# Placing three steps of a two-layer mLSTM and RG-LRU trunk by TensorE time, and turning one tile without DRAM

## The chip, the core and the metric

The kernel runs on one core of one Trainium2 chip. A core has a matrix engine (TensorE, PE in the profile), a vector engine (VectorE, DVE), an engine for pointwise functions (ScalarE, ACT), a general engine (GpSimd, POOL) and SyncE (SP), which here does nothing but issue transfers. Each engine works through its own queue in order. The metric is the device time of one execution in microseconds, as the median of several runs.

## The reference

The input `x` has 256 tokens of 2048 channels in float32. Two layers follow one another, then a root-mean-square norm. A layer does this:

```
u = rms_norm(x, norm_g);  p = u @ w_in            # 2048 -> 2048*6 + 16 columns
qk, v, o, z_a, ig, fg, xb, z_b = split(p)
qk = silu(causal_dwconv(qk, qk_conv))             # 4 taps along the tokens
h  = mlstm(q, k, v, ig, log_sigmoid(fg))          # 8 heads, dk 128, dv 256
h  = head_norm(h * sigmoid(o)) ;  y_a = h * silu(z_a)
xc = causal_dwconv(xb, lru_conv_w) + lru_conv_b
y_b = rg_lru(xc) * silu(z_b)                      # 8 blocks of 256 channels
x  = x + concat(y_a, y_b) @ w_out                 # 4096 -> 2048
```

In `mlstm` the weight of token s in the output at token t is (q_t . k_s) times exp(F_t - F_s + i_s - m_t), where F is the running sum of the log forget gate and m a running maximum; the sum over s is divided by max(|its sum without v|, exp(-m_t)). The kernel computes it over all 256 tokens at once, as a causal matrix of decays, `E`, times the scores. `rg_lru` makes two gates from `xc` by two block-diagonal products and then runs a linear recurrence h_t = a_t h_(t-1) + u_t along the tokens.

## The kernel before, in words

**Products.** All large products are weight streams. The weights lie in DRAM in blocks; a *unit* is 1 MB, a *half* 512 KB. For each half, SyncE loads a tile `raw` (128 x 1024), ScalarE casts it to `wH` (a rounded copy for the matrix engine), VectorE subtracts to get the rest `wL`, and TensorE multiplies the activations, themselves kept as a rounded part and a rest, in three products: rounded by rounded, rounded by rest, rest by rounded. A half of the ordinary kind is 12 matmuls of 128 x 128 by 512 columns. The loop at the end of `tile_trunk` goes over all halves in order; at half `n` it has prepared (cast and split) the halves up to `n + 3` (`AHEAD`). There are eight `raw` buffers (`SLOTS`) and four each of `wH` and `wL`. Some input products are done blockwise with sums of weights (`block_halves`, lines 1234 to 1236); their halves are 6 matmuls.

**Groups.** A layer goes in four groups `g` of two heads and 512 LRU channels. For each group the columns of q and k (`qk`), `v`, `o`, `z`, `xb` and `zb` are computed, then the two gate products of the LRU; the output product of a group comes while the next group is computed. In layer 1 the last group's output product is a function of its own, `last_out`: the rows of `w_out` in four quarters, of which the first two multiply `y_a` (lines 1357 to 1359 with `yaH`, `yaL`), the last two `y_b` (`ybH`, `ybL`). The third quarter's weights are cast into a tile of their own, `w_own`, and the casts are ordered behind those that make `ybH` and `ybL`.

**Turns.** The products give tokens on the partitions; the convolutions and the recurrence need channels there. `to_channels` copies a product into `tok` (ScalarE), `swapped` transposes it in 32 x 32 blocks into `blk` (VectorE, line 532), then four transfers issued by SyncE write it into a DRAM tile `moved` (line 535) in another order of blocks, and one transfer brings it back as `fr` (line 536). That one is issued by GpSimd, except for the last turn of all, `zb` of group 3 in layer 1, which SyncE issues: `zb_post` passes `back = nc.sync` there.

**The order of the work around the products.** Everything between the products is written as Python generators in a list `bg`. After each half the function `pump` goes through the list and asks each for its next step. A step yields its estimated cost, which is added to a lag; at a lag of 3 us (`FULL`) the pass ends. A generator that yields "wait" is passed over until the next pass. `st["t"]` counts the TensorE time of the halves so far, 2.72 us for an ordinary half and 1.36 us for a blockwise one, and `before(t)` is true until that clock has reached `t`. `require` runs steps by force when a product needs their result. So it is this clock that places a step between the casts and splits on ScalarE and VectorE; `order(...)` ties a step behind the newest cast or split. Within these ties, and those of the data, a scheduler of the framework settles the order on each engine, by its own estimate of when things are ready. Where an engine reaches an instruction whose input isn't there, it waits, and all that is queued behind it too.

The steps that the change touches:

- `e_gen` (lines 652 to 675) makes `E` of a group. It issues the transfer of two rows of `nG_d` to all partitions (`nb`, line 657, by GpSimd), yields "wait" four times, waits for `aT`, then lets VectorE add and clip (four instructions, lines 666 and 667), ScalarE take the exponential (line 669) and GpSimd set the upper triangle to zero (line 672).
- `qk_post` (from line 709): at least 10 us (`LANDING`) of TensorE time behind the turn, ScalarE copies `fr` to the tile `ch` (`joined`), the convolution runs over it (a ScalarE instruction and three on VectorE for each of four channel tiles, giving `qc`), a sigmoid and a product follow, and later the scores: products `ps_S` (lines 754 and 756) on TensorE, copied and added to `Pt`, times `E`. `Pt` lies in the buffer of `ch`; the flag `st["ch"]` says that it is in use. There are three small PSUM tiles (`aux`), and the scores of a head need two.
- `xb_post` (from line 838): the LRU channels, likewise at least 10 us behind their turn and when `ch` is free: `joined`, convolution to `xc`, and after the scores its cast and split.
- `zb_post` (line 933): the turned `zb` gives a sigmoid (`zsg`), two products and then `ybH` and `ybL`.

Of the kernel before, what the change touches and what calls it, by code (L numbers as in the profile page):

```python
# [22 lines left out]
NG = 4  # L23
# [3 lines left out]
O_NG, O_HG, O_QKW, O_LW, O_LB, O_BA, O_BX, O_LAM, NPAR = 0, 16, 32, 96, 160, 176, 192, 208, 224  # L27
AHEAD = 3
LANDING = 10.0
FAR = 15.0  # L30
BORDER = 7
BLANKS = 7
# [67 lines left out]
def tile_trunk(ctx, tc, x, xt, par, gw, gb, ws, final_g, out):  # L100
    nc = tc.nc
    G, PE = nc.gpsimd, nc.tensor
# [27 lines left out]
    st = {"nload": 0, "lag": 0.0, "dma": 0.0, "t": 0.0, "rate": RATE[0], "nprep": 0, "pair": 0, "aux": 0}  # L130
# [84 lines left out]
    def tt_(o, a, b, op):  # L215
        return V.tensor_tensor(out=o, in0=a, in1=b, op=op)
# [4 lines left out]
    def ts_(o, a, s1, op0, s2=None, op1=None):  # L221
        if s2 is None:
            return V.tensor_scalar(out=o, in0=a, scalar1=s1, scalar2=None, op0=op0)
        return V.tensor_scalar(out=o, in0=a, scalar1=s1, scalar2=s2, op0=op0, op1=op1)
# [45 lines left out]
    def order(ins, prev):  # L270
        tc.add_manual_dep(ins.ins, prev.ins.name,
                          mybir.DependencyInfo(mybir.DependencyClass.NoSync, mybir.DependencyReason.DATA),
                          reason="an order of the program")
# [28 lines left out]
    def before(t):  # L302
        return st["t"] < t and not st.get("forced")

    def pause(g, us, waits):
        t = st["t"] + us
        while before(t) if g < NG - 1 else waits > 0:
            waits -= 1
            yield "wait"
# [189 lines left out]
    def conv(x_, o, ct, wcol, l, bias):  # L499
        wv = pars[:, l, wcol : wcol + 4]  # L500
        if bias is None:
            S.activation(out=o[:, ct, :], in_=x_[:, ct, :], func=AF.Copy, scale=wv[:, 3:4])
        else:
            S.activation(out=o[:, ct, :], in_=x_[:, ct, :], func=AF.Identity, scale=wv[:, 3:4], bias=bias)
        for d in (1, 2, 3):
            stt(o[:, ct, d:T], x_[:, ct, 0 : T - d], wv[:, 3 - d : 4 - d], o[:, ct, d:T], ALU.mult, ALU.add)
# [8 lines left out]
    def to_channels(l, acc, back=G):  # L515
        require(("rstd", l))
        rstd = st["rstd", l]
        tok = new_tok()
        for t in range(2):
            S.activation(out=by_block(tok, t), in_=acc[:, t, :].rearrange("p (c m j) -> p c m j", c=4, m=4),  # L520
                         func=AF.Copy, scale=rstd[:, t : t + 1])
        return swapped(tok, back=back)

    def swapped(tok, blk=None, back=G):


        if blk is None:
            blk = work.tile([P, 4, 256], F32, tag="blk", name="blk")
        fr = work.tile([P, 4, 4, 2, 32], F32, tag="fr", name="fr", bufs=2)
        st["lag"] += 1.2  # L530
        st["dma"] += TURN
        V.transpose(out=blk.rearrange("p m n -> p (m n)"), in_=tok.rearrange("p m c t j -> p (m c t j)"))
        moved = dram.tile([P, 4, 256], F32, tag="moved", name="moved", bufs=2)
        for a in range(4):
            nc.sync.dma_start(out=moved[:, a].rearrange("(m j) n -> j m n", m=4), in_=blk[32 * a : 32 * a + 32])
        i0 = back.dma_start(out=fr.rearrange("p a c t i -> p a (c t i)"), in_=moved)  # L536
        if back is G:
            st["gq"] = i0
        return fr

    def pieces(fr):
# [15 lines left out]
    def joined(fr):  # L557
        ch = work.tile([P, 4, T], F32, tag="ch", name="ch")
        order(S.copy(out=whole(ch), in_=pieces(fr)), st["wH"])
        return ch  # L560
# [91 lines left out]
    def e_gen(l, g):  # L652
        while ("nG", l) not in st:
            yield "wait"
        nb = work.tile([P, 2, T], F32, tag="sD", name="nb")
        src = nG_d[l][2 * g : 2 * g + 2, :].rearrange("h t -> (h t)").partition_broadcast(P)
        st["nb", l, g] = nc.gpsimd.dma_start(out=nb.rearrange("p h t -> p (h t)"), in_=src)
        for _ in range(4):
            yield "wait"
        while ("aT", l) not in st:  # L660
            yield "wait"
        E = small.tile([P, 2, 384], F32, tag="E", name="E", bufs=1)
        aT = st["aT", l]
        for h in range(2):
            hd = 2 * g + h
            ts_(E[:, h, 0:256], nb[:, h, :], aT[:, 0, hd : hd + 1], ALU.add, 0.0, ALU.min)
            ts_(E[:, h, 256:384], nb[:, h, 128:256], aT[:, 1, hd : hd + 1], ALU.add, 0.0, ALU.min)
        yield 0.7
        order(S.activation(out=E, in_=E, func=AF.Exp), st["wH"])
        for h in range(2):  # L670
            for o in (0, 256):
                G.affine_select(out=E[:, h, o : o + 128], in_=E[:, h, o : o + 128], pattern=[[1, 128]],
                                compare_op=ALU.is_ge, fill=0.0, base=0, channel_multiplier=-1)
        st["E", l, g] = E
        yield 0.1
# [32 lines left out]

    def qk_post(l, g, acc):
        bg.append(e_gen(l, g))  # L710
        fr = to_channels(l, acc)
        relaxed = 0 < g < NG - 1
        t0 = st["t"]

        def gen():
            while before(t0 + LANDING) or st.get("ch"):
                yield "wait"
            st["turning"] = st["ch"] = True
            ch = joined(fr)
# [3 lines left out]
            for ct in range(4):  # L723
                conv(ch, qc, ct, O_QKW + 4 * (8 * (ct % 2) + 2 * g + ct // 2), l, None)
                yield 1.45
            st["ch"] = False
            if relaxed:
                yield "wait"
            order(S.activation(out=sg, in_=qc, func=AF.Sigmoid), st["wH"])
# [11 lines left out]
            st["turning"] = False  # L741
            yield 1.2
            yield from pause(g, 7.0, 3)
            while any((k, l, g) not in st for k in ("E", "v", "so")) or st["ch"]:
                yield "wait"
            st["ch"] = True
            E, em, so, (vH, vL) = st["E", l, g], st["em", l], st["so", l, g], st["v", l, g]
# [27 lines left out]
            for h in range(2):  # L775
                pns = [aux("ps_n") for _ in range(2)]
                for t in range(2):
                    o = pns[t][:, 0:258]
                    a = slice(P * t, P * t + P)
# [23 lines left out]
            st["hn", l, g] = hh  # L803
            yield 1.0
        bg.append(gen())

    def z_post(l, g, acc, sign="rstd"):
# [13 lines left out]
        def gen():  # L821
# [8 lines left out]
            t0 = st["t"]  # L830
            while before(t0 + (FAR if g < NG - 1 else LANDING)):
                yield "wait"
# [5 lines left out]
    def xb_post(l, g, acc):  # L838
        fr = to_channels(l, acc)
        t0 = st["t"]  # L840

        def gen():
            while before(t0 + LANDING) or st["ch"]:
                yield "wait"
            st["ch"] = True
            ch = joined(fr)
            yield 0.3
            xc = work.tile([P, 4, T], F32, tag="c4", name="xc", bufs=2)
            for ct in range(4):
                tix = 4 * g + ct  # L850
                conv(ch, xc, ct, O_LW + 4 * tix, l, pars[:, l, O_LB + tix : O_LB + tix + 1])
                yield 1.45
            st["ch"] = False
            while ("scores", l, g) not in st:
                yield "wait"
            xs = work.tile([P, 4, 2, T], F32R, tag="xcs", name="xcs")
            for b in range(2):
                sl_ = slice(2 * b, 2 * b + 2)
                S.copy(out=xs[:, sl_, 0, :], in_=xc[:, sl_, :])
                tt_(xs[:, sl_, 1, :], xc[:, sl_, :], xs.bitcast(F32)[:, sl_, 0, :], ALU.subtract)  # L860
                yield 0.6
            st["xc", l, g] = (xc, xs)
        bg.append(gen())
# [69 lines left out]
    def zb_post(l, g, acc):  # L933
# [4 lines left out]
        def gen():  # L938
            while not ending and before(t0 + FAR):
                yield "wait"  # L940
# [68 lines left out]
    def gate_before(l, g):  # L1009
        require(("xc", l, g))  # L1010
        if g == NG - 1:
            load_x_acc()

    def out_chunk(l, g, c):
# [9 lines left out]
        def postfn():  # L1024
# [27 lines left out]
            if c < 3:  # L1052
                tt_(xs, xs, ps, ALU.add)
            fr = swapped(tok, blk)
            square_sum(c)
            store_x(c)
# [391 lines left out]
    for item in dict.fromkeys(i for i, _ in seq):  # L1448
        kind, l, g = item[0], item[1], item[-1]
# [5 lines left out]
        elif kind == "gate":  # L1455
            add_unit([gate_half(l, g, 0), gate_half(l, g, 1)],
                     before=lambda l=l, g=g: gate_before(l, g), after=lambda l=l, g=g: gate_post(l, g))
# [6 lines left out]
    for item, j in seq:  # L1464
        l, what = item[1], item[2:]
        if _blockwise(item):
            p = next(p for p in range(PRODUCTS[l]) if what in PAIRS[p])
# [5 lines left out]
    for l in reversed(range(DEPTH)):  # L1473
        for p in reversed(range(PRODUCTS[l])):
            a, b = ends[l, p - 1], ends[l, p]
            if p == 1:
                g = PAIRS[1][1][1]
# [139 lines left out]
```

## Time and profile before

| | |
|---|---|
| median of 3 runs | 1478.61 us (1477.98 to 1481.65) |
| the profiled execution | 1479.07 us, of which 1477.2 us lie between its first and last instruction |
| TensorE busy | 1460.8 us (99%), 6734 matmuls |
| VectorE, ScalarE busy | 1213.1 us (82%), 981.5 us (66%) |
| GpSimd busy | 129.5 us (9%) |
| DMA | 417.06 MB, 282 GB/s on average |

In the rows of the profile, "L413" is line 413 of the kernel; where a helper records an operation its line stands for all of its callers (line 114 for nearly all of VectorE and ScalarE), so the tile names tell more: `acc<-wH,x_s` is a product of the tiles `wH` and `x_s` into `acc`. "x2" counts merged instructions. A figure in brackets, such as [2.75 <-DVE wL L114], is the time that the engine sat idle before the row, and what ended it. SPq and POOLq are the queues of SyncE and GpSimd. TensorE overlaps one matmul with the next, and the ends of matmuls are modelled: rows that are 0.39 us long may start 0.23 us apart.

### The profile page before, as it was taken

The numbers are of one execution on the slowest core, as the hardware profiler recorded it, in microseconds if no ns is written. First come the engines' busy times: TensorE is split into PE (matmuls) and PEld (weight loads), VectorE is DVE, ScalarE is ACT, GpSimd is POOL, SyncE is SP. The second block draws the span as 40 slices with busy tenths as digits, with TensorE's granted clock in tenths as the row PEclk, the third lists the DMA queues.
The fourth block names the chain that finished last, engine by engine and source line by source line (L and its number), as shares of the span: only waits on it lengthen the run. The fifth ranks groups of instructions, "written<-read, shape, count | busy, mean of one in ns | idle before, by whom it ended". The sixth has DMA issues, their size and how long they took to land.

```text
span 1477.2 us, 19595 instructions
## 1 busy us (share of the span) xinstructions
PE 1460.8 (99%) x6734; PEld 1217.2 (82%) x6734; DVE 1213.1 (82%) x1710; ACT 981.5 (66%) x1255; POOL 129.5 (9%) x210
## 2 busy tenths in 40 slices
PE   9999999999999999999999999999999999999997
PEld 7888888888888888888888788888888788888885
DVE  6888898878888699888857789988787877998875
ACT  7666766568676666668665577655677756667774
POOL 0020110110100000100100201111000000000002
PEclk9999999999999999999999999999999999999999
DMA  9979999999989998988998888999988899888891
GB/s 343 337 242 283 284 315 292 309 252 330 348 288 257 289 335 286 303 250 285 293 301 258 229 277 275 292 299 275 316 263 295 251 261 286 307 287 269 232 342 60
DMA packets 158708, 417.06 MB, mean 282 GB/s; under 512 B 14848, under 2 KB 35344, under 8 KB 158608
## 3 DMA queue, kind: packets, MB, share of 16 engines
q1 hardware_dynamic: 136432, 340.01, 67.7%
q0 software_dynamic: 19712, 71.33, 21.1%
q10 hardware_dynamic: 2464, 4.47, 0.8%
q8 instruction: 53, 0.87, 0.2%
q14 instruction: 47, 0.39, 0.1%
HBM read 378.50 MB, written 74.99 MB: 307 GB/s over the span
## 4 chain that ended last, share of the span: by engine, by line
PE 86%; DMA 6%; DVE 4%; issue 3%; ACT 1%; SPq 0%; POOL 0%; POOLq 0%; DVEq 0%; ACTq 0%
PE acc L413 68%; PE ps_b L1234 3%; PE ps_b L1236 3%; PE ps_b L1235 3%; PE ps_gt L879 3%; DMA raw<-in_ws_dram 2%; DMA fr<-moved 2%; PE acc L426 2%; DMA moved<-blk 1%; DVE wL L114 1%; DVE xc L114 1%; DVE qc L114 1%; PE acc L1358 1%; PE acc L1359 1%; PE acc L1357 1%
## 5 line engine op out<-in xcount | busy, mean ns | idle before, releaser
L114 DVE TENSOR_TENSOR wL<-raw,wH 128x1024 fp32r<-128x1024 f32 (+1 forms) x580 | 692.8, 1202 | 187.1 <-ACT wH L114 185.2
L114 ACT CAST wH<-raw 128x1024 fp32r<-128x1024 f32 (+1 forms) x580 | 597.2, 1039 | 356.1 <-PE acc L413 250.2
L413 PE MATMUL acc<-wH,x_s 128*128 128x512 f32 x2496 | 783.7, 389 | 0.0
L413 PEld LDWEIGHTS acc<-wH,x_s 128*128 128x128 f32 x2496 | 468.3, 188 | 97.6 <-ACT wH L114 1.1
L413 PE MATMUL acc<-wL,x_s 128*128 128x512 f32 x1248 | 484.7, 389 | 3.0 <-DVE wL L114 3.0
L413 PEld LDWEIGHTS acc<-wL,x_s 128*128 128x128 f32 x1248 | 234.3, 188 | 51.9 <-DVE wL L114 4.1
L413 PE MATMUL acc<-wL,ybH 128*128 128x512 f32 x224 | 87.3, 390 | 0.6 <-DVE wL L114 0.6
L413 PE MATMUL acc<-wH,ybL 128*128 128x512 f32 x224 | 87.5, 390 | 0.3 <-DVE ybL L989 0.3
L413 PE MATMUL acc<-wH,ybH 128*128 128x512 f32 x224 | 87.6, 391 | 0.0
L413 PE MATMUL acc<-wH,yaH 128*128 128x512 f32 x224 | 87.4, 390 | 0.0
L413 PE MATMUL acc<-wL,yaH 128*128 128x512 f32 x224 | 87.2, 389 | 0.0
L413 PE MATMUL acc<-wH,yaL 128*128 128x512 f32 x224 | 87.2, 389 | 0.0
L114 ACT ACT_TABLE_LOAD x62 | 79.5, 1283 | 5.1 <-DVE qc L114 2.7
L1141 POOL DMA_DIRECT2D w_d<-in_ws_dram x64 | 48.9, 765 | 292.8 <-ACT wH L114 265.4
L536 POOL DMA_DIRECT2D fr<-moved x34 | 19.2, 566 | 511.3 <-DMA moved<-blk 450.9
L114 DVE SCALAR_TENSOR_TENSOR xc<-ch,pars,xc 128x255 f32<-128x255 f32 (+2 forms) x96 | 42.3, 477 | 10.3 <-ACT xc L114 10.0
L1234 PE MATMUL ps_b<-wH,sums 128*128 128x512 f32 x128 | 50.1, 391 | 0.0
L413 PEld LDWEIGHTS acc<-wH,ybL 128*128 128x128 f32 x224 | 42.1, 188 | 9.7 <-DVE ybL L989 1.0
L1236 PE MATMUL ps_b<-wH,sums 128*128 128x512 f32 x128 | 49.9, 390 | 0.0
L1235 PE MATMUL ps_b<-wL,sums 128*128 128x512 f32 x128 | 49.9, 390 | 0.0
L413 PEld LDWEIGHTS acc<-wL,ybH 128*128 128x128 f32 x224 | 42.1, 188 | 9.3 <-DVE wL L114 0.9
L413 PEld LDWEIGHTS acc<-wH,yaL 128*128 128x128 f32 x224 | 42.0, 188 | 8.8
(229 smaller groups left out, 1763.2 us busy)
## 6 DMA issues: line engine op xcount, KB each, us to landing
raw<-in_ws_dram SPq DMA_DIRECT2D x542, 512.0 KB, 6.7
w_d<-in_ws_dram POOLq DMA_DIRECT2D x64, 512.0 KB, 9.1
raw<-w_d SPq DMA_DIRECT2D x48, 512.0 KB, 6.7
fr<-moved POOLq DMA_DIRECT2D x34, 512.0 KB, 7.3
moved<-blk SPq DMA_DIRECT2D x132, 128.0 KB, 3.9
x_d<-stage POOLq DMA_DIRECT2D x24, 512.0 KB, 7.9
x_d<-x_acc ACTq DMA_DIRECT2D x8, 512.0 KB, 7.8
w_d<-w_d POOLq DMA_DIRECT2D x8, 512.0 KB, 7.0
```

Of the source, the lines that this page charges most:

```text
L114: ins = f(*a, **k)
L413: st["mm"] = PE.matmul(o, a_[:, kt, P * t : P * t + P], W[:, k], start=b, stop=z)
L426: PE.matmul(ps[:, ct, T * part : 2 * T], W[:, k, P * ct : P * ct + P], moving, start=first and k == 0 and part == 0, stop=last and k == 3 ...
L536: i0 = back.dma_start(out=fr.rearrange("p a c t i -> p a (c t i)"), in_=moved)
L879: PE.matmul(o, W[:, ib, jl], xs[:, ib, a, :], start=j == 0 and i == 0 and W is Hv and a == 0, stop=i == 1 and W is Lv, skip_group_check=True)
L1141: i0 = G.dma_start(out=wd[l][p][to][j][:, cs], in_=(wd[l][p][src][j] if src == 0 else block_unit(l, p, *src, j))[:, cs], **how)
L1234: PE.matmul(box["b"], aH, Hv[:, k], start=opening and k == 0, stop=False, skip_group_check=True)
L1235: PE.matmul(box["b"], aH, Lv[:, k], start=False, stop=False, skip_group_check=True)
L1236: PE.matmul(box["b"], aL, Hv[:, k], start=False, stop=kp == 3 and k == 1, skip_group_check=True)
L1357: PE.matmul(o, yH[:, kt, tsl], Hv[:, k, cs], start=start and k == 0, stop=False)
L1358: PE.matmul(o, yH[:, kt, tsl], Lv[:, k, cs], start=False, stop=False)
L1359: PE.matmul(o, yL[:, kt, tsl], Hv[:, k, cs], start=False, stop=stop and k == 1)
```

## The change

There are four edits.

1. The four passes that `e_gen` waited become a wait by TensorE time: 10 us behind the issue of `nb`, 16 us in group 0.
2. When a convolution (of q and k or of the LRU channels) has been issued, the time is noted with 4 us added (`SETTLED`). In groups 0 to 2 the scores wait for that time.
3. The LRU channels' join and convolution of groups 1 and 2 begin 12.7 us behind their turn, not 10.
4. The last turn no longer goes through DRAM: 16 transfers, issued by SyncE, each take 32 partitions of 1 KB from `blk` straight to `fr`. All other turns stay as they were.

```diff
 LANDING = 10.0
+SETTLED = 4.0
...
         V.transpose(out=blk.rearrange("p m n -> p (m n)"), in_=tok.rearrange("p m c t j -> p (m c t j)"))
+        if back is not G:
+            for m in range(4):
+                for a in range(4):
+                    back.dma_start(out=fr[32 * m : 32 * m + 32, a].rearrange("p c t i -> p (c t i)"),
+                                   in_=blk[32 * a : 32 * a + 32, m])
+            return fr
         moved = dram.tile([P, 4, 256], F32, tag="moved", name="moved", bufs=2)
         for a in range(4):
             nc.sync.dma_start(out=moved[:, a].rearrange("(m j) n -> j m n", m=4), in_=blk[32 * a : 32 * a + 32])
-        i0 = back.dma_start(out=fr.rearrange("p a c t i -> p a (c t i)"), in_=moved)
-        if back is G:
-            st["gq"] = i0
+        st["gq"] = G.dma_start(out=fr.rearrange("p a c t i -> p a (c t i)"), in_=moved)
         return fr
...
         st["nb", l, g] = nc.gpsimd.dma_start(out=nb.rearrange("p h t -> p (h t)"), in_=src)
-        for _ in range(4):
-            yield "wait"
-        while ("aT", l) not in st:
+        t0 = st["t"]
+        while before(t0 + (LANDING if g > 0 else 1.6 * LANDING)) or ("aT", l) not in st:
             yield "wait"
...
-            st["ch"] = False
+            st["ch"], st["ch_t"] = False, st["t"] + SETTLED
             if relaxed:
                 yield "wait"
             order(S.activation(out=sg, in_=qc, func=AF.Sigmoid), st["wH"])
...
-            while any((k, l, g) not in st for k in ("E", "v", "so")) or st["ch"]:
+            while any((k, l, g) not in st for k in ("E", "v", "so")) or st["ch"] or g < NG - 1 and before(st["ch_t"]):
                 yield "wait"
...
-            while before(t0 + LANDING) or st["ch"]:
+            while before(t0 + (LANDING + 2.7 if 0 < g < NG - 1 else LANDING)) or st["ch"]:
                 yield "wait"
             st["ch"] = True
             ch = joined(fr)
...
-            st["ch"] = False
+            st["ch"], st["ch_t"] = False, st["t"] + SETTLED
             while ("scores", l, g) not in st:
                 yield "wait"
```

## The prediction

> **What bounds the kernel now.** I read the page first, then what TensorE (PE) waited for, then PE's timeline at each of those waits, and last the engine that each wait points to.
>
> ```profile
> PE 1460.8 (99%) x6734; PEld 1217.2 (82%) x6734; DVE 1213.1 (82%) x1710; ACT 981.5 (66%) x1255; POOL 129.5 (9%) x210
> ```
> ```profile
> PE acc L413 <- DVE wL L114: 3.6, 3, 2.8
> PE ps_S L754 <- DVE Pt L114: 1.5, 2, 0.8
> PE ps_blank L146 <- DVE blank L114: 1.3, 1, 1.3
> PE acc L1357 <- ACT w_own L114: 0.9, 2, 0.5
> PE acc_x L1357 <- ACT w_own L114: 0.4, 1, 0.4
> PE acc L413 <- DVE ybL L989: 0.3, 1, 0.3
> ```
>
> PE is busy for 99% of the span and the change takes no matmul away, so all that can be won is PE's own waiting: the rows (total, times, longest) sum to 8.0 us, of which 1.3 lie in the opening and 0.3 at a tile that the change leaves alone. PE's timeline shows where the rest is, and that a wait costs more than its idle figure.
>
> ```profile
> 826.40 0.61 PE L413 MATMUL acc<-wH,x_s 128*128 128x512 f32 x2
> 829.77 0.50 PE L413 MATMUL acc<-wL,x_s 128*128 128x512 f32 x1 [2.75 <-DVE wL L114]
> ```
> ```profile
> 445.00 0.39 PE L754 MATMUL ps_S<-qks 128*128 128x256 f32 x1 [0.76 <-DVE Pt L114]
> ```
> ```profile
> 1171.85 0.50 PE L413 MATMUL acc<-wL,ybH 128*128 128x512 f32 x1 [0.58 <-DVE wL L114]
> 1177.17 0.39 PE L754 MATMUL ps_S<-qks 128*128 128x256 f32 x1 [0.78 <-DVE Pt L114]
> ```
> ```profile
> 1444.14 0.39 PE L1358 MATMUL acc_x<-wL,yaH 128*128 128x512 f32 x1
> 1444.37 0.39 PE L1359 MATMUL acc_x<-wH,yaL 128*128 128x512 f32 x1
> 1445.17 0.49 PE L1357 MATMUL acc<-w_own,ybH 128*128 128x512 f32 x1 [0.41 <-ACT w_own L114]
> ```
>
> Undisturbed matmuls start 0.23 us apart (1444.14, 1444.37) though each is drawn 0.39 long, so an idle of g loses g + 0.16, and the first matmul behind it is drawn 0.50 instead of 0.39, another 0.11. A wait costs its idle and 0.27. That makes 3.02 at 829.77 (layer 1, group 0), 1.03 at 445.00 (layer 0, group 2), 0.85 and 1.05 at 1171.85 and 1177.17 (layer 1, group 2), and 1.3 + 3 x 0.27 = 2.1 at the three waits on w_own, from 1445.17 on (the end). Together 8.1 us. The fourth short wait on wL (3.6 less 2.75 and 0.58, about 0.3) belongs to none of the edits.
>
> **E, the decay matrix (lines 658 to 668).** Who holds VectorE (DVE) up before 829.77:
>
> ```profile
> 821.13 5.96 DMA nb<-nG_d
> ```
> ```profile
> 820.43 1.21 DVE L114 TENSOR_TENSOR wL<-raw,wH 128x1024 fp32r<-128x1024 f32 x1
> 827.18 1.01 DVE L114 TENSOR_SCALAR E<-nb,at 128x256 f32<-128x256 f32 x4 [5.54 <-DMA nb<-nG_d]
> ```
> ```profile
> 828.22 0.84 ACT L114 ACTIVATE E<-E 128x768 f32<-128x768 f32 x1 [5.78 <-DVE E L114]
> ```
>
> E stands in DVE's order behind the weight split of 820.43 and waits there 5.54 us for nb, which lands at 827.1; the next split is queued behind E, and PE waits for it. The old rule was four passes of the planner, one for each half unit of 12 matmuls, which it counts as 2.72 us of PE time: 10.9 us; the new one in group 0 is 16 us, reached at the sixth pass. E therefore moves behind two more splits. Two splits of 1.21 from 821.6 end at 824.1; E still waits, from there to 827.1, and ends at 828.2. PE, not held up, wants these splits at 826.9 and 829.6, and the third at 832.3. With about 0.5 us of convolution and 1.2 of split behind E, the third is there at 829.9: 2.4 us early. So the 3.0 us go although DVE still idles. Cover gone: ScalarE (ACT) would do E's exponential, a table load, a sigmoid and only then the third cast; 0.84 + 1.28 + 1.06 + 1.05 (the last three from the rows of the end, below) and 1.2 for the split, from 828.2 on, end at 833.7, a new wait of 1.4 us. So 1.6 to 3.0; I take 3.0, because PE frees the buffer for that cast at 824.1, one pass ahead of 826.9, while the exponential can't begin before 828.2.
>
> ```profile
> DVE E L114 <- DMA nb<-nG_d: 5.5, 1, 5.5
> ```
> ```profile
> ACT wH L114 <- PE acc L413: 250.2, 173, 5.4
> ```
>
> This was the only E of eight that waited for nb. For the other seven the new floor is 10 us instead of four passes; where passes were skipped because the planner's lag was full, E may now come earlier than before, elsewhere one pass later. Each moves 1.0 us on DVE and 0.84 with a table load on ACT. What hides it: ACT sits idle 250.2/173 = 1.4 us before such casts because the four weight buffers are full. I take nothing; without that cover one E could cost about 1 us, and some could also gain a little. No queue is passed: nb is issued where it was.
>
> **The LRU channels and the scores in group 2 (lines 843, 726, 744).** Layer 1, ACT and then DVE:
>
> ```profile
> 1160.53 2.00 ACT L114 CAST wH<-raw 128x1024 fp32r<-128x1024 f32 x2
> 1165.58 1.05 ACT L114 COPY ch<-fr 128x1024 f32<-128x1024 f32 x1 [3.04 <-DMA fr<-moved]
> 1168.15 1.04 ACT L114 CAST wH<-raw 128x1024 fp32r<-128x1024 f32 x1
> 1175.76 0.54 ACT L114 COPY Pt<-ps_S 128x256 f32<-128x256 f32 x2 [3.23 <-DVE xc L114]
> ```
> ```profile
> 1167.30 3.37 DVE L114 SCALAR_TENSOR_TENSOR xc<-ch,pars,xc 128x255 f32<-128x255 f32 x8 [3.32 <-ACT xc L114]
> 1170.58 1.22 DVE L114 TENSOR_TENSOR wL<-raw,wH 128x1024 fp32r<-128x1024 f32 x1
> ```
> ```profile
> 433.41 1.05 ACT L114 COPY ch<-fr 128x1024 f32<-128x1024 f32 x1 [2.16 <-DMA fr<-moved]
> ```
>
> ACT stands 3.04 us (2.16 in layer 0) in front of the turned channels with a cast queued behind them; DVE idles 3.32 and then must do convolution and splits in one row. The split of 1170.58 is late by what 1171.85 shows. The scores' copy Pt shares the tile `ch` with the convolution and waits 3.23 for it, and PE's second pair of score products waits for Pt. LANDING + 2.7 puts the join one pass later (2.72, or 1.36 where a pass is half as long): one cast goes ahead of it. That cast and its split, 1.04 + 1.22, fit into the 3.04 and 3.32 us in which both engines idled, if PE frees the buffer early in them, as it does once in a pass; the split is then there about 1166, against PE's need at 1171.1 (1171.85 less 0.58 and 0.16). ACT's wait shrinks to 1 to 2 us and costs nothing. DVE's convolution keeps its end or comes 1.2 us sooner, by the split that no longer lies in it. The scores then wait 4 us of PE time behind the last convolution step, one or two passes in addition: their first products move by 4 to 5 us, to when Pt's tile is free or nearly (it was free at 1175.8). So 0.85 + 1.05 + 1.03 = 2.9 us go. If the convolution only moves along with the scores, nothing is won; if a different split falls behind it, that costs what 1171.85 cost, 0.85 in each layer. Range -1.7 to 2.9, and I take 2.9, since it is idle time of 3.3 us that is filled. What is later: numerators, the normalized heads and the gates' input; the gates of this group stand some 55 us behind (in layer 1 the scores at 1177, the gates' products at 1232.9).
>
> ```profile
> 1232.91 4.20 PE ps_gt L879 x36
> ```
>
> In group 1, where the rules hold too, PE waits for none of these steps, and group 3 is left out of both: nothing.
>
> **The last turn (lines 533 to 538).** Removed: four transfers to DRAM and one back, with a wait in SyncE's (SP's) queue between. Added: sixteen of a quarter of the size.
>
> ```profile
> 1426.52 1.84 SPq L535 DMA_DIRECT2D moved<-blk  x4
> 1428.45 1.82 SPq L360 DMA_DIRECT2D raw<-in_ws_dram  x2
> 1432.50 0.33 SPq L536 DMA_DIRECT2D fr<-moved  x1
> ```
> ```profile
> 1436.63 1.05 ACT L114 CAST wH<-raw 128x1024 fp32r<-128x1024 f32 x1 [1.67 <-PE acc L1359]
> 1437.71 1.28 ACT L114 ACT_TABLE_LOAD   x1
> 1439.00 1.06 ACT L114 ACTIVATE zsg<-fr 128x1024 f32<-128x1024 f32 x1
> 1443.04 1.14 ACT L114 CAST ybH<-zb 128x512 fp32r<-128x512 f32 x2
> 1444.08 3.89 ACT L114 CAST w_own<-raw 128x1024 fp32r<-128x1024 f32 x4
> ```
> ```profile
> raw<-in_ws_dram SPq DMA_DIRECT2D x542, 512.0 KB, 6.7
> moved<-blk SPq DMA_DIRECT2D x132, 128.0 KB, 3.9
> ```
>
> An issue takes 1.84/4 = 0.46 us, sixteen take 7.4, so the last one begins at about 1433.4 and lands, by the 3.9 of the nearest row, at 1437.3. Before, `fr` was issued at 1432.50 and had landed by 1439.0. The turn is some 1 to 1.7 us sooner. The sigmoid zsg did not wait for it: it ran straight behind its table load, which ran straight behind the cast of 1436.63, which waited for PE. So with ACT's order unchanged the end gains nothing. But that cast belongs to the last quarter of the output product and is written far behind zsg; the order on ACT follows an estimate of when things are ready, and an earlier turn may put zsg ahead of it. Then ybH and the w_own casts move up by a pass or nearly and the 2.1 us go. I take the middle, 1.0. The cost: two raw loads stand behind the sixteen, so the second, issued at 1429.9 (1428.45 + 1.82, less an issue of about 0.35), goes to about 1434.3 and lands, by the 6.7 of its row, at 1441.0 instead of 1436.6. If its cast still stands ahead of zsg, the end is late; that is a rival.
>
> Sum: 3.0 + 2.9 + 1.0 = 6.9 us off the profiled execution's 1479.07, that is 1472.2. That execution lies 0.46 above the median of 1478.61, so the forecast for the median is 1471.7.
>
> **The rivals.**
>
> *The waits move on.* E's exponential blocks a cast (1.4 us back), and the group 2 burst shifts as a whole with its stalls (2.9 not won), while the end gives its 1.0 or nothing. Gain 1.6 to 2.6: about 1476.5. For it: DVE is 82% busy and fills up again behind every burst. Against: the idle of 3.3 us directly before the burst. The case in which the new rules hardly change the order is this one too.
>
> *The late raw load.* ACT's order stays and the cast of 1436.63 waits for its load. With an issue time d the load lands at 1426.9 + 16d + 6.7; cast 1.05, table 1.28, zsg 1.06, a product of this size 1.22 (as the split of 1170.58), ybH 1.14 and one w_own cast 1.04 put PE's third quarter at 1440.4 + 16d, against 1445.2 now. At d = 0.46 that is 1447.8, a loss of 2.6: 1478.6 - 5.9 + 2.6 = 1475.3, within 0.3%.
>
> *Slower.* The same chain with dearer issues or transfers that queue up: the 5.9 us are eaten at d = 0.67, and the kernel is slower by 0.3% from d = 0.94. The longest single issue of this kind took 1.18, the median 0.44.
>
> ```profile
> L535 SPq DMA_DIRECT2D moved<-blk x132: 303/435/1178, 59.0 to 1427.8; - x132
> ```
>
> At d = 1.18 PE begins the quarter 14 us late: 1478.6 - 5.9 + 14.1 = 1486.8. The rows speak against it: the four of 1426.52 had all landed when `fr` was issued 6.0 us later, so they overlapped. [...]
>
> **How the numbers follow.** A measurement of this kernel can tell about 0.3%, 4.4 us, from no change: faster means below 1474.2, slower above 1483.0. Forecast 0.62, waits that move on 0.18, late raw load 0.13, slower 0.07. The upper edge of the forecast's own spread and the lower edge of the late load lie on either side of 1474.2 and about cancel; I give faster 0.64, same 0.29, slower 0.07. Range: at the low end all 8.1 us and about 1 us of luck with the other E's, 1469.5; at the high end the second case with the upper part of its spread, 1477.0.
>
> **What would show it.** Right: no PE wait on wL above 0.3 us near 830 (E's own DVE wait shrinks to about 3), none on Pt; ACT's wait for fr before ch in group 2 below 1.5; zsg ahead of the cast that now precedes it, and the waits on w_own gone or smaller. Wrong: PE waiting for wL beside E in other groups, a wait of 0.8 or more left in group 2, a cast waiting for raw at the end, or more than 8 us for the sixteen issues.

## The result and the profile after

| | us |
|---|---|
| before, median of 4 runs beside the changed kernel | 1479.32 (1477.98 to 1481.65) |
| after, median of 4 runs | 1495.79 (1493.87 to 1496.80) |
| ratio, 95% interval | 1.0108 (1.0091 to 1.0126) |
| forecast | 1471.7 (1469.5 to 1477.0) |
| profiled execution after: time, span | 1493.87, 1492.2 |

The kernel became 16.5 us slower, where 6.9 faster was forecast, and the time lies far above the range.

PE's list of waits in the changed kernel comes first (total, times, longest):

```profile
PE acc L414 <- DVE wL L115: 7.3, 3, 3.5
PE acc L1361 <- ACT w_own L115: 2.7, 1, 2.7
PE ps_b L1238 <- ACT wH L115: 2.2, 2, 1.1
PE ps_b L1239 <- DVE wL L115: 1.5, 2, 0.8
...
PE acc L1362 <- DVE w_own L115: 1.1, 1, 1.1
```

The waits on `Pt` are gone, as forecast. New are two waits of 3.5 us for `wL`, four in front of products into `ps_b`, and longer ones for `w_own`. A table of PE's losses by stretch tells where they lie. For each matmul it takes the distance to the start of the next one, less 0.227 us per 512 columns, which is the spacing of undisturbed matmuls; what is left above zero is summed over the stretch. Each line is one profiled execution; the kernels below the second line are the experiments.

| kernel | whole span | 400-500 (layer 0, group 2) | 800-850 (E, layer 1, group 0) | 1150-1250 (layer 1, group 2) | behind 1400 (end) |
|---|---|---|---|---|---|
| before | 19.1 | 1.4 | 3.5 | 2.4 | 2.4 |
| after | 34.0 | 8.6 | 0.2 | 9.9 | 6.4 |
| E_rule_alone | 31.3 | 9.6 | 0.2 | 8.8 | 2.5 |
| E_group2_alone | 35.0 | 9.3 | 1.6 | 9.9 | 3.3 |
| swap_alone | 31.6 | 7.4 | 1.3 | 9.7 | 2.5 |
| xb_scores_alone | 21.4 | 0.3 | 4.5 | 0.9 | 2.5 |
| after_pinned | 20.6 | 0.3 | 0.2 | 0.5 | 7.7 |
| turn_alone | 21.3 | 1.1 | 2.0 | 1.6 | 6.7 |
| turn_loads_aside | 22.3 | 0.3 | 1.5 | 2.4 | 7.4 |
| turn_two_queues | 13.8 | 0.3 | 1.7 | 1.5 | 0.2 |
| E0_xb_scores | 16.2 | 0.3 | 0.2 | 0.5 | 2.3 |
| E0_xb_two_queues | 11.7 | 0.3 | 0.2 | 0.5 | 0.2 |
| after_repaired | 11.7 | 0.8 | 0.2 | 1.2 | 0.2 |

From before to after the whole grows by 14.9 us, and the spans differ by 15.0: 7.2 and 7.4 us more in the two groups 2 (before rounding), 4.0 more at the end, and 3.3 less at E.

**E.** PE's timeline of the changed kernel at the place of the old wait:

```profile
829.66 0.39 PE L414 MATMUL acc<-wL,x_s 128*128 128x512 f32 x1
```

No wait stands there, and DVE's wait of E for `nb` fell from 5.5 to 2.3 us, with weight splits ahead of it:

```profile
832.32 1.01 DVE L115 TENSOR_SCALAR E<-nb,at 128x256 f32<-128x256 f32 x4 [2.27 <-DMA nb<-nG_d]
```

This step went as forecast.

**Group 2.** PE's timeline in layer 1 (layer 0 has the same rows around 443 and 450):

```profile
1177.92 0.50 PE L1238 MATMUL ps_b<-wH,x_s 128*128 128x512 f32 x1 [1.11 <-ACT wH L115]
1179.18 0.51 PE L1239 MATMUL ps_b<-wL,x_s 128*128 128x512 f32 x1 [0.76 <-DVE wL L115]
...
1185.05 0.80 PE L414 MATMUL acc<-wL,yaH 128*128 128x512 f32 x1 [3.47 <-DVE wL L115]
1185.64 0.63 PE L414 MATMUL acc<-wH,yaL 128*128 128x512 f32 x1
1186.07 0.63 PE L414 MATMUL acc<-wH,yaH 128*128 128x512 f32 x1
```

The split that PE wants comes from DVE, whose timeline says why it is late:

```profile
1177.90 1.23 DVE L115 TENSOR_TENSOR wL<-raw,wH 128x1024 fp32r<-128x1024 f32 x1 [8.26 <-ACT wH L115]
1179.04 4.82 DVE L115 SCALAR_TENSOR_TENSOR xc<-ch,pars,xc 128x255 f32<-128x255 f32 x12
1183.77 4.63 DVE L115 TENSOR_TENSOR wL<-raw,wH 128x1024 fp32r<-128x1024 f32 x4
```

DVE idles 8.3 us for a cast (before, it idled 3.3 us here, for ACT's step of the convolution), and then the whole convolution stands in one row ahead of the splits. ACT's timeline shows what held up the cast:

```profile
1163.25 1.02 ACT L115 COPY stage<-acc 128x1024 f32<-128x1024 f32 x1 [1.62 <-PE acc L414]
...
1167.33 1.05 ACT L115 CAST wH<-raw 128x1024 fp32r<-128x1024 f32 x1 [1.17 <-PE acc L414]
1175.88 1.05 ACT L115 COPY ch<-fr 128x1024 f32<-128x1024 f32 x1 [7.49 <-DMA fr<-moved]
1176.83 1.04 ACT L115 CAST wH<-raw 128x1024 fp32r<-128x1024 f32 x1
```

The join `ch<-fr` does stand one cast later (the third cast, of 1167.33), as forecast. But `fr` is so late that the join waits 7.5 us instead of 3.0, and the cast of 1176.83, for which DVE idles, stands behind it. The last step back is GpSimd's timeline, of the kernel before and of the changed one:

```profile
1156.45 0.56 POOL L536 DMA_DIRECT2D fr<-moved  x1 [21.07 <-DMA moved<-blk]
1160.94 0.89 POOL L1029 DMA_DIRECT2D x_d<-stage  x1 [3.93 <-ACT stage L114]
```
```profile
1164.57 0.89 POOL L1033 DMA_DIRECT2D x_d<-stage  x1 [22.84 <-ACT stage L115]
1165.23 0.79 POOL L543 DMA_DIRECT2D fr<-moved  x1
```

The two transfers have changed places. The return of the turned channels now stands behind the adding transfer of the last group's output; that one waits until ACT has copied `stage` (1163.25 + 1.02), and so `fr` is issued at 1165.2 and no longer at 1156.5. On PE's work, which lies 3.9 us later in the changed kernel here (7.2 less 3.3), this is 4.9 us late. The join is 6.4 us late by the same count, since `fr` then also takes longer to land (last section).

**The end.** SyncE's, ACT's and PE's timelines of the changed kernel:

```profile
1437.60 10.96 SPq L537 DMA_DIRECT2D fr<-blk  x16
1448.66 2.78 SPq L361 DMA_DIRECT2D raw<-in_ws_dram  x5
```
```profile
1450.25 1.28 ACT L115 ACT_TABLE_LOAD   x1 [4.22 <-DMA fr<-blk]
...
1455.48 1.05 ACT L115 CAST wH<-raw 128x1024 fp32r<-128x1024 f32 x1 [2.87 <-DMA raw<-in_ws_dram]
...
1457.47 3.88 ACT L115 CAST w_own<-raw 128x1024 fp32r<-128x1024 f32 x4
```
```profile
1458.56 0.50 PE L1361 MATMUL acc<-w_own,ybH 128*128 128x512 f32 x1 [2.74 <-ACT w_own L115]
1460.17 0.58 PE L1362 MATMUL acc<-w_own,ybH 128*128 128x512 f32 x1 [1.11 <-DVE w_own L115]
```

The sixteen issues take 10.96 us instead of the 7.4 of the forecast. The sigmoid did move ahead of the cast of the last quarter, as the prediction hoped; but it now waits 4.2 us for `fr`, and behind it the cast waits 2.9 us for a `raw` whose load was queued behind the sixteen.

### The profile page after: what moved, and what is told of

Read it like the earlier page. It is cut to its first block, busy times and chain, and to the rows that moved or that the text cites. A ratio compares the mean times of both kernels' runs of the same rounds, so it can differ in the third digit from the quotient of the medians.

```text
span 1492.2 us, 19617 instructions
## 1 busy us (share of the span) xinstructions
PE 1467.1 (98%) x6734; PEld 1221.7 (82%) x6734; DVE 1214.3 (81%) x1710; ACT 981.1 (66%) x1255; POOL 139.1 (9%) x210
## 4 chain that ended last, share of the span: by engine, by line
PE 91%; DMA 3%; DVE 3%; ACT 1%; SPq 1%; issue 1%; DVEq 0%; ACTq 0%; POOLq 0%
PE acc L414 75%; PE ps_b L1238 3%; PE ps_b L1240 3%; PE ps_b L1239 3%; PE ps_gt L883 2%; DMA raw<-in_ws_dram 2%; DVE wL L115 1%; DVE xc L115 1%; DMA moved<-blk 1%; SPq L537 1%; PE ps_g L593 0%; DMA fr<-moved 0%; PE ps_blank L147 0%; PE ps_n L684 0%; PE ps_n L682 0%
## 5 line engine op out<-in xcount | busy, mean ns | idle before, releaser
L414 PEld LDWEIGHTS acc<-wL,yaH 128*128 128x128 f32 x224 | 43.1, 192 | 16.5 <-DVE wL L115 7.8
L414 PEld LDWEIGHTS acc<-wH,yaH 128*128 128x128 f32 x224 | 43.0, 192 | 10.1 <-ACT wH L115 1.4
```

The lines of the kernel that those rows point to most:

```text
L414: st["mm"] = PE.matmul(o, a_[:, kt, P * t : P * t + P], W[:, k], start=b, stop=z)
```

## The experiments

Two theories stood at the start. The queue theory: E's new rule puts the E of group 2 one half later, this turns the two transfers in GpSimd's queue, and that is the loss in both groups 2; the last turn loses 4 us of its own. The placement theory: the later join and the later scores are what makes group 2 late. In the table, each difference is from the median of before in the runs beside it.

| kernel | us | from before | ratio (95%) |
|---|---|---|---|
| E_rule_alone | 1491.11 | +13.9 | 1.0093 (1.0080 to 1.0106) |
| xb_scores_alone | 1476.04 | -1.2 | 0.9990 (0.9978 to 1.0001) |
| turn_alone | 1481.10 | +3.8 | 1.0028 (1.0017 to 1.0040) |
| E_group2_alone | 1492.77 | +15.5 | 1.0101 (1.0086 to 1.0115) |
| after_pinned | 1480.09 | +1.5 | 1.0012 (1.0000 to 1.0023) |
| E0_xb_scores | 1475.30 | -3.3 | 0.9983 (0.9973 to 0.9993) |
| turn_loads_aside | 1481.57 | +3.0 | 1.0026 (1.0015 to 1.0036) |
| turn_two_queues | 1476.76 | -1.8 | 0.9988 (0.9976 to 1.0001) |
| swap_alone | 1491.82 | +14.3 | 1.0096 (1.0078 to 1.0113) |
| E0_xb_two_queues | 1471.87 | -5.7 | 0.9964 (0.9950 to 0.9978) |
| after_repaired | 1471.74 | -5.8 | 0.9961 (0.9947 to 0.9976) |

**E_rule_alone**: the first edit alone.

```
-        for _ in range(4):
-            yield "wait"
-        while ("aT", l) not in st:
+        t0 = st["t"]
+        while before(t0 + (LANDING if g > 0 else 1.6 * LANDING)) or ("aT", l) not in st:
```

> The kernel before with the new rule for E alone (all eight E's). Measure: before is 1479.3. Queue theory: in the changed kernel the idle time of PE beyond the steady spacing of its matmuls grew by 7.2 us in layer 0, group 2 and by 7.4 in layer 1, group 2, because the E of group 2, one half unit later, turns the order of two transfers in GpSimd's queue (the adding output transfer x_d<-stage now ahead of the return fr<-moved of the LRU channels). Then this kernel has both stalls (PE waits on wL of about 3.6 beside 450 and 1185) and lacks the wait at 829.77: 1479.3 - 3.3 + 14.6 = 1490.6. Placement theory (the rival): the stalls come from joining the channels one half unit later and the scores 4 us later; then this kernel has none of them and only the gain at 829.77: 1476.0.

It is 13.9 us slower, 2.6 more than the queue theory's 11.3, and far from the placement theory's gain. Both groups 2 have their stalls, with no edit to join or scores in the kernel. The long waits aren't the ones that the expectation named, of 3.6 us for `wL`; PE stands in front of its score products:

```profile
PE ps_S L753 <- DVE Pt L114: 8.9, 2, 4.4
```

E_group2_alone and swap_alone, which have the old scores too, show such waits on `Pt`, of 3.3 to 4.4 us.

**xb_scores_alone**: the second and third edit alone.

```
-            while before(t0 + LANDING) or st["ch"]:
+            while before(t0 + (LANDING + 2.7 if 0 < g < NG - 1 else LANDING)) or st["ch"]:
...
-            while any((k, l, g) not in st for k in ("E", "v", "so")) or st["ch"]:
+            while any((k, l, g) not in st for k in ("E", "v", "so")) or st["ch"] or g < NG - 1 and before(st["ch_t"]):
```

> The kernel before with the later join of the LRU channels (LANDING + 2.7 in groups 1 and 2) and the scores' wait of 4 us alone; E and the last turn as before. Queue theory: GpSimd's order is that of before, fr<-moved lands where it landed (1165.6 in layer 1), no stall of 3.6 us: between the 2.9 us that the prediction gave these edits and nothing, 1476.4 to 1479.3. Placement theory: both stalls, 1479.3 + 14.6 = 1493.9.

The median is 1.2 us lower, with an interval that just reaches no change. ACT's timeline in layer 1:

```profile
1168.92 1.05 ACT L115 COPY ch<-fr 128x1024 f32<-128x1024 f32 x1 [2.59 <-DMA fr<-moved]
```

No PE wait is left in either group 2 (table: 0.3 and 0.9 against 1.4 and 2.4). These two edits do what they were forecast to do; the placement theory falls. Most of what is left in this execution are the 4.5 us at E, which this kernel doesn't move, and 4.4 us around 340, where ACT stood 5.7 us in front of a cast whose `raw` load was late, which no other profile here has at that size.

**E_group2_alone**: the new rule for E in group 2 alone, the other six E's as before.

```
+        t0, waits = st["t"], 0 if g in (2,) else 4
-        for _ in range(4):
+        while waits > 0:
+            waits -= 1
             yield "wait"
-        while ("aT", l) not in st:
+        while g in (2,) and before(t0 + (LANDING if g > 0 else 1.6 * LANDING)) or ("aT", l) not in st:
```

> The kernel before with the new rule for E in group 2 alone, of both layers: two of eight E's, each one half unit later. Queue theory: this single move turns the two transfers in GpSimd's queue and gives both stalls, with nothing won at 829.77: 1479.3 + 14.6 = 1493.9, ACT's join ch<-fr waiting about 7 us instead of 3.0 in layer 1. Placement theory: an E moved by one half unit costs nothing: 1479.3.

Two E's moved by one half cost 15.5 us, which is the queue theory's figure within the scatter.

**swap_alone** separates E's move from the order that follows it. E stays; one order is added to the kernel before.

```
         fr = to_channels(l, acc)
+        st["xbq"] = st["gq"], g
...
                 st["gq"] = G.dma_start(out=xd[c], in_=stage, accum_op=ALU.add)
+                if c == 0 and g == 1 and st["xbq"][1] == 2:
+                    order(st["xbq"][0], st["gq"])
```

> The kernel before with one order added: in group 2 of each layer the return fr<-moved of the LRU channels stands behind the first adding output transfer x_d<-stage in GpSimd's queue. No rule of the planner is changed, E stands where it stood. Queue theory: both stalls, 13 to 16 us above before, as with the E of group 2 moved. Rival: it takes E's move as well (its 1.0 us on DVE and 0.84 on ACT in front of the LRU channels): nothing or a few us.

GpSimd's and ACT's timelines in layer 1:

```profile
1166.08 0.91 POOL L1030 DMA_DIRECT2D x_d<-stage  x1 [25.56 <-ACT stage L114]
1166.74 0.79 POOL L536 DMA_DIRECT2D fr<-moved  x1
```
```profile
1178.12 1.05 ACT L114 COPY ch<-fr 128x1024 f32<-128x1024 f32 x1 [8.22 <-DMA fr<-moved]
```

The order alone costs 14.3 us, with no E moved. It is enough for the loss.

**after_pinned** is the other half: the changed kernel whole, with the two transfers held in the old order.

```
         fr = to_channels(l, acc)
+        st["xbq"] = st["gq"]
...
                 st["gq"] = G.dma_start(out=xd[c], in_=stage, accum_op=ALU.add)
+                if c == 0:
+                    order(st["gq"], st["xbq"])
```

> The changed kernel whole, with one order added: in each group the first adding output transfer (x_d<-stage, column block 0) stays behind the return fr<-moved of the LRU channels in GpSimd's queue, as before; all else as changed. Queue theory: both stalls of group 2 go (14.6 us), and what is left is E's gain in group 0, the 2.5 us that the later join and scores won when they ran alone, and the loss at the end (turn_alone: +3.8): within 0.2% of the kernel before, from 1.5 us below it to 2 above. Rival: the order of the two transfers is only a companion of the late LRU channels, and E's new place in ACT's and DVE's order is what holds them up: then the time stays 14 to 16 us above before.

```profile
1155.41 0.56 POOL L543 DMA_DIRECT2D fr<-moved  x1 [19.36 <-DMA moved<-blk]
1158.90 0.88 POOL L1034 DMA_DIRECT2D x_d<-stage  x1 [2.93 <-ACT stage L115]
```
```profile
1163.94 1.05 ACT L115 COPY ch<-fr 128x1024 f32<-128x1024 f32 x1 [1.23 <-DMA fr<-moved]
```

All E's moved, and the stalls are gone: 0.3 and 0.5 us in the two groups 2, the join waiting 1.2 us, and the time 1.5 us above before. With swap_alone this settles group 2: the order in GpSimd's queue is the cause, and E's move matters only by turning it.

**turn_alone**: the last turn's sixteen transfers alone.

```
+        if back is not G:
+            for m in range(4):
+                for a in range(4):
+                    back.dma_start(out=fr[32 * m : 32 * m + 32, a].rearrange("p c t i -> p (c t i)"),
+                                   in_=blk[32 * a : 32 * a + 32, m])
+            return fr
```

> The kernel before with the last turn's sixteen transfers from SBUF to SBUF alone. The changed kernel lost 4.0 us of PE time behind 1400. Issue theory: the sixteen issues take SyncE about 0.65 us each, 10.5 to 11 us in all against the 7.4 of the prediction, fr is no sooner, and the raw loads behind them land some 9 us late, so that the cast of the last quarter waits for raw and holds ybH and w_own up: 1479.3 + 4.0 = 1483.3. Rival: the loss at the end is a follower of the late group 2 (loads and lag shifted), and the turn by itself gives its forecast gain: 1478.3.

It costs 3.8 us by itself, so the loss at the end is no follower of group 2. SyncE's and ACT's timelines:

```profile
1424.57 11.13 SPq L536 DMA_DIRECT2D fr<-blk  x16
1435.79 2.67 SPq L360 DMA_DIRECT2D raw<-in_ws_dram  x5
```
```profile
1437.11 1.28 ACT L114 ACT_TABLE_LOAD   x1 [4.33 <-DMA fr<-blk]
...
1443.01 1.04 ACT L114 CAST wH<-raw 128x1024 fp32r<-128x1024 f32 x1 [3.55 <-DMA raw<-in_ws_dram]
```

An issue costs 11.13/16 = 0.70 us. The first three edits and this one add up: 13.9 - 1.2 + 3.8 = 16.5, the whole loss.

**turn_loads_aside** takes the weight loads behind the turn out of SyncE's queue.

```
         if back is not G:
+            st["late"] = True
...
-            st["ld"] = nc.sync.dma_start(out=raw, in_=ws[blocks[item, j]][:, 1024 * i : 1024 * i + 1024])
+            st["ld"] = (G if st.get("late") else nc.sync).dma_start(out=raw, in_=ws[blocks[item, j]][:, 1024 * i : 1024 * i + 1024])
```

> turn_alone with one thing more: the six weight loads (raw) that follow are issued by GpSimd, whose queue is empty there, and no longer by SyncE behind the sixteen. Late-load theory: the 3.6 us that ACT's cast waits for raw in front of ybH go, PE's wait on w_own shrinks from 3.7 to 0.5 or less, and the +3.8 us of turn_alone become -1 to +1 against before. Late-turn theory: fr itself is what comes late (issue by issue, 11 us), ybH waits for zsg and not for the cast, and the +3.8 stay. ACT's, DVE's and PE's orders are those of turn_alone.

```profile
1440.89 1.28 ACT L114 ACT_TABLE_LOAD   x1 [7.87 <-DMA fr<-blk]
...
1443.15 1.03 ACT L114 CAST wH<-raw 128x1024 fp32r<-128x1024 f32 x1
```

The late-load theory failed in its number: the loss stays, +3.0, as the late-turn theory of the expectation has it. The cast no longer waits for `raw`, but the table load in front of `zsg` waits 7.9 us for `fr` instead of 4.3, so the wait only changed its place. From issue to landing one of the sixteen took 4.2 to 7.2 us with the loads beside it (median 5.4), and 1.8 to 4.4 in turn_alone (median 2.8). So neither order of the loads saves the turn while eleven us of issues stand in one queue.

**turn_two_queues** halves the queue.

```
-                    back.dma_start(out=fr[32 * m : 32 * m + 32, a].rearrange("p c t i -> p (c t i)"),
+                    (back if m < 2 else G).dma_start(out=fr[32 * m : 32 * m + 32, a].rearrange("p c t i -> p (c t i)"),
```

> turn_alone with eight of the sixteen transfers issued by GpSimd and eight by SyncE. If the issue on one queue is the price (0.70 us each), SyncE is done after 5.6 us, fr is there some 5 us sooner than in turn_alone, the loads behind are in time, and the end gains instead of losing: 1 to 2 us below before. If the price lies in the transfers themselves (32 KB each, queueing up on the DMA engines), fr is as late as in turn_alone and the end loses about as much (+2 to +4). Beside this, zsg comes to stand ahead of two more casts in ACT's order, so that a late fr would hold up more than it did.

SyncE's, GpSimd's and ACT's timelines:

```profile
1423.40 5.04 SPq L536 DMA_DIRECT2D fr<-blk  x8
```
```profile
1423.66 3.96 POOL L536 DMA_DIRECT2D fr<-blk  x8 [6.33 <-DVE blk L114]
```
```profile
1430.80 1.28 ACT L114 ACT_TABLE_LOAD   x1 [1.68 <-DMA fr<-blk]
1432.09 1.06 ACT L114 ACTIVATE zsg<-fr 128x1024 f32<-128x1024 f32 x1
...
1434.44 1.15 ACT L114 CAST ybH<-zb 128x512 fp32r<-128x512 f32 x2 [0.35 <-DVE zb L114]
```

The two queues issue side by side, 5.0 and 4.0 us. The table load runs 6.3 us earlier than in turn_alone, PE waits for nothing behind 1400, and the same sixteen transfers no longer cost anything: 1.8 us below before, with an interval that just reaches no change, where one queue lost 3.8. The time of issue fell from 11.1 to 5.0 us, while a transfer took no less time to land (median 3.6 us, 2.8 in turn_alone), so the price lay in the issue on one queue.

**E0_xb_scores** keeps E's new rule for group 0 only, with the two edits of xb_scores_alone.

```
+        t0 = st["t"]
-        for _ in range(4):
-            yield "wait"
-        while ("aT", l) not in st:
+        if g > 0:
+            for _ in range(4):
+                yield "wait"
+        while g == 0 and before(t0 + 1.6 * LANDING) or ("aT", l) not in st:
```

> The kernel before with what the queue theory says is worth keeping: E's new rule for group 0 alone (the four passes for groups 1 to 3), the later join and the scores' wait; the last turn as before. Queue theory: no stall in group 2, no PE wait on E near 830; by the medians of the first four runs (E_rule_alone less E_group2_alone, -1.6; xb_scores_alone, -1.2) 2.8 us below before, by the excesses that the traces show (3.3 and 2.5) up to 5.8 below. Rival: what is won at 830 and in group 2 is lost behind it, no difference.

It is 3.3 us faster than before, between the two sums of the expectation; the whole interval lies below no change.

**E0_xb_two_queues** and **after_repaired** put the parts together: the first is E0_xb_scores and the second after_pinned, each with the sixteen issued from two queues by the diff of turn_two_queues.

> E's new rule for group 0 alone, the later join and the scores' wait, and the last turn's sixteen issued half by GpSimd and half by SyncE. If the three gains add up: -3.3 (E0_xb_scores) and -1.8 (turn_two_queues), 5 us below before; if the end's gain is only what the profiles show (2.2 us of PE waits), 5.5 below. Rival: they share what they win, 3 us below.

> The changed kernel whole, E's new rule for all groups, with the two transfers of GpSimd's queue in the order of before and the sixteen issued half by GpSimd. If E's new place costs nothing in groups 1 to 3 once the queue is in order, it is as fast as the kernel that moves E in group 0 alone, 4 to 5.5 us below before; if the moved E's cost something of their own, it lies above that by as much (up to 1 us for each of six).

PE's waits of after_repaired:

```profile
PE ps_blank L147 <- DVE blank L115: 1.3, 1, 1.3
PE acc L414 <- DVE wL L115: 0.4, 2, 0.3
PE acc L414 <- ACT wH L115: 0.3, 1, 0.3
```

Both are faster than before and than the changed kernel, by 5.7 and 5.8 us from before, and they are alike: E's in groups 1 to 3 may stand one half later for nothing, once the queue is in order. Behind the opening PE waits 0.7 us in all. That 1471.74 lies beside the forecast's 1471.7 is chance: before stood at 1477.52 in these runs, and the written order and the second queue are not part of the change that was forecast.

## Why the prediction was wrong, point by point

**E in group 0** was right in its mechanism: the wait is gone and DVE's wait for `nb` shrank to 2.3 us ("about 3"). Its size was read from an execution with a long wait. Two kernels that leave this E alone, turn_alone and swap_alone, show at the same place:

```profile
828.41 0.50 PE L413 MATMUL acc<-wL,x_s 128*128 128x512 f32 x1 [1.22 <-DVE wL L114]
```
```profile
834.90 0.50 PE L413 MATMUL acc<-wL,x_s 128*128 128x512 f32 x1 [0.57 <-DVE wL L114]
```

In the table the seven executions without the new rule in group 0 lose 1.3 to 4.5 us in that stretch, 2.3 in the mean, against 0.2 with it: the term is 2.1, not 3.0. One of the seven, xb_scores_alone, lost the most behind a wait shorter than the one before (2.39 against 2.75 us); the last section tells why.

**The other seven E's**: here the prediction failed, at "I take nothing" and "No queue is passed: nb is issued where it was." It asked which queue E's own transfer passes and what E's instructions hide, and never asked which other instructions change places when E moves. The order on each engine follows an estimate of readiness, as the prediction itself wrote of ACT at the end; a new place for one step can reorder transfers that it has nothing to do with. E_group2_alone shows it: +15.5 us, and swap_alone gives 14.3 of them with no E moved.

**Group 2** was right for its two edits and wrong for their surroundings. "ACT's wait shrinks to 1 to 2 us" came true in after_pinned (1.2), and no wait on `Pt` is left. The size, again from one execution, was high: the four profiled kernels with the old join and the old queue (before and the three with only the turn changed) lose 1.8 to 3.8 us in the two stretches, 2.8 in the mean, and the five with the edits and that queue 0.8 to 2.0, 1.1 in the mean: some 1.7 instead of 2.9. The measured time of xb_scores_alone says 1.2. The assumption that `fr` lands when it landed was never stated as one, though the rest hung on it. Of the rivals, the burst that "shifts as a whole with its stalls" came nearest, but the dearest case that the prediction saw in group 2 was 0.85 us in each layer; it had no transfer that comes later.

**The last turn**: the order on ACT changed as taken, and the term is mis-sized in its first factor. The issue was put at 0.46 us, from four transfers to DRAM of four times the size; it is 0.69 in the changed kernel. So `fr` was there no sooner than by way of DRAM: the table load in front of `zsg` waits for it until 12.7 us behind the first issue (1437.60 to 1450.25), where before it began, without waiting, 11.2 us behind the first issue (1426.52 to 1437.71), and the 1.0 us became -4.0 in the profile. The rival "late raw load" named the cast that then waited, and the prediction's sign of being wrong, "more than 8 us for the sixteen issues", was met. But that rival kept ACT's order, and it missed that the sixteen land later with loads beside them (turn_loads_aside: a median of 5.4 us from issue to landing, 2.8 in turn_alone), so that either `raw` or `fr` is late. The sixteen did not pay their time to land in turn: its median is 2.6 us in the changed kernel, which makes 42 us for sixteen, and all had landed 12.7 us behind the first issue.

**The rival "slower"** was given 0.07 and a mechanism at the end alone, where it asked for d, the time of one issue, above 0.94. The kernel was slower through a queue in the middle that no rival named.

**The sum.** The terms were put at -3.0 (E in group 0), -2.9 (group 2), -1.0 (the last turn) and 0 (the other E's). The runs give about -2.1 (the table), -1.2 (xb_scores_alone), +3.8 (turn_alone) and +15.5 (E_group2_alone), which makes 16.0 of the 16.5 us.

**What stays open**: why the program's order puts `x_d<-stage` ahead of `fr<-moved` when E of group 2 moves by one half. That it does, and what it costs, is shown; the estimate behind it isn't seen in a profile. It is also open why `fr` takes longer to land where it stands behind `x_d<-stage`.

## What to carry to other kernels

When a step moves in a program whose queues are ordered by estimates, list for every queue the transfers that stand beside its new and old place, and read in the profile which of two neighbours may not wait for the other: a transfer that waits for an evacuation must not stand ahead of one that a chain waits for (swap_alone: +14.3 us), and an order written out cost nothing that after_repaired shows. The sixteen small transfers were priced by issue time times count in one queue (0.70 us each in turn_alone, +3.8 us; 5.0 us of issue on two queues, -1.8); spread such transfers over queues that are idle there. Waits picked from one profiled execution are picked because they were long; size their removal by several.

## What the runs showed of the hardware that was not expected

PE runs slowly behind some of its waits. After the wait of 3.47 us matmuls start 0.43 us apart (1185.64, 1186.07) instead of 0.23, and the granted clock of those stretches of the changed kernel (columns: length, PE busy, clock, DMA share, GB/s) says why:

```profile
1185.60:1190.00 4.40, 4.40 (x12) 0.50 0.93 216
```
```profile
1191.00:1195.00 4.00, 4.00 (x19) 1.00 0.98 365
```

From 1185.05 to 1190.44 PE starts work worth 2.8 us at its usual spacing and needs 5.4, so the wait costs 2.6 us beyond its own length. At the end two waits of 2.7 and 1.1 us with a single matmul between them were enough for the same spacing (0.43 us between the matmuls of 1460.55 and 1463.54, at a clock of 0.50). The prediction's price, idle and 0.27, held for the wait of 2.75 us before, behind which the clock stayed at 1.00 from 830 to 835. It did not hold for a shorter wait, at the same place in xb_scores_alone:

```profile
832.20 0.50 PE L414 MATMUL acc<-wL,x_s 128*128 128x512 f32 x1 [2.39 <-DVE wL L115]
```
```profile
833.30:836.60 3.30, 3.30 (x9) 0.50 0.86 282
```

So the length of a wait alone doesn't decide. In the changed kernel the granted clock was 0.50 from 450.11 to 453.52, from 1183.98 to 1190.80 and from 1460.46 to 1463.87, that is for 3.41, 6.83 and 3.41 us, and 1.00 between; in each of the thirteen traces the steps of the clock lie whole multiples of 3.41 us apart. Divide a trace at these steps into stretches of 3.41 us and add up PE's idle time in each: up to PE's last matmul the clock was halved behind all fourteen full-clock stretches with 2.0 to 3.4 us of idle time (3.4, 2.65 and 2.6 in the changed kernel), and behind none with 1.75 or less. The 2.75 us before lay across a border, 1.0 on one side and 1.75 on the other; the 2.39 us of xb_scores_alone lay within one stretch, and the two waits at the end of the changed kernel share one, with 2.6 us in it. It was luck, then, that the wait of 2.75 us before cost no more than the prediction's price. Most of the fourteen stretches weren't idle as a whole; 2.0 us in one were enough. What sets their length, and what would have followed between 1.75 and 2.0 us, the runs don't show.

`fr` also lands later behind an adding transfer: it took from 1156.45 to ACT's start of the join at 1165.58, 9.1 us, before, and from 1165.23 to 1175.88, 10.7 us, behind `x_d<-stage`. In group 2 of both layers it took, in the four kernels with the turned order, 9.0 to 11.4 us from issue to landing, 10.5 in the mean, and in the nine others 6.7 to 9.2, 8.2 in the mean. The runs don't separate what makes it later.
